# Stick-breaking attention of a hybrid layer: from one query block at a time to steps of two

## The chip, the cores and the metric

The kernel runs on one core of one Trainium2 chip. The metric is the device time of one execution in microseconds (us); lower is better. The core has five engines with an instruction queue each, which meet through semaphores: TensorE (PE in the profile; PEld is its loading of weights), VectorE (DVE), ScalarE (ACT), GpSimd (POOL) and SyncE (SP), which here issues the DMAs. TensorE writes its products to PSUM, and the other engines read them from there.

## What is computed

One layer on 1024 tokens with 16 meta tokens ahead of them, 1024 wide. A normalised input is projected to an SSD mixer and to an attention of 16 heads of 64; both outputs are normalised and go through one W_out of 2048 rows, and a gated feed-forward part follows.

```python
proj = xn @ w_in[l]
...
y_ssd = ssd_mixer(z, xbc, dt_raw, ...)
y_sb = rms_norm(stick_breaking_attention(q, k, v).reshape(Bsz, L, SB_WIDTH), sb_norm_g[l])
mix = jnp.concatenate([y_ssd, y_sb], axis=-1) @ w_out[l]
h = h + rms_norm(mix, mix_post_g[l])
...
f = (jax.nn.gelu(g, approximate=True) * gu[..., D_FF:]) @ w_down[l]
h = h + rms_norm(f, ffn_post_g[l])
```

The attention has no softmax. A key takes the share beta of what the keys after it have left over:

```python
valid = (key_pos[None, :] < q_pos[:, None]) & (key_pos[None, :] >= pad)
zlog = jnp.einsum('bqhd,bkhd->bhqk', qi, kp) * scale
log_beta = jax.nn.log_sigmoid(zlog)
log_keep = jnp.where(valid, log_beta - zlog, 0.0)
after = lax.cumsum(log_keep, axis=3, reverse=True) - log_keep
w = jnp.where(valid, jnp.exp(log_beta + after), 0.0)
return jnp.einsum('bhqk,bkhd->bqhd', w, vp)
```

## The kernel before

The stages follow each other: the input and its projections, the SSD mixer, attention, the output projection, the feed-forward part. The change is in attention and at its seams to the output projection.

Attention runs over eight head pairs `p` (two heads of 64 side by side on TensorE) and, in each, over eight blocks of 128 queries in the order `BLOCKS = (7, 0, 6, 1, 5, 2, 4, 3)`, so that a long block and a short one alternate. Block `i` sees n = 16 + 128(i+1) keys. What is done for one block:

- *Scores*, `block_weights`: q and k are split in a high and a low part, and a score is three products for each head of the pair (z, L1277), in chunks of at most 512 keys (`key_chunks`). ScalarE makes the sigmoid (L1278), and VectorE runs a scan over the keys from the last to the first (L1281), one for each head and chunk, with `hold` as the causal mask. The result is `kp`, what a key leaves over. There are three buffers for long blocks and three for short ones.
- *Corner*, `corner_copy` (L1256): GpSimd puts the first 16 queries' columns of the meta keys' end aside in `cb`.
- *Turns*, `block_turn`, of the block three places earlier (`TURN_LAG`): TensorE transposes `kp` in pieces of 128 keys (tw, L1298); ScalarE copies them as 1-x to `th` (L1303; four buffers).
- *Values*, `block_mix`: products of v and `th` (av, L1316), copied by ScalarE into the head pair's output `ysc` (L1319).
- *Pieces* (`do`): TensorE work from elsewhere, put between the steps above. First come the last pieces of the q and k projections (`plain_steps`, L219; six products of 260 columns each), then the halo rows (`halo_rows`, L1436: two output rows that the convolution further on needs, from the split high and low parts of W_out and in eight rows of four products of 512 columns), then the output projection of the SSD half (`out_steps`, mo, L1471; six products of 512 columns a piece, 64 pieces). `shares`, `FILL_AT` and `OUT_FILL` share a fixed number of pieces out over the 64 blocks; the rest runs after the loop.
- *Edge*, once for each head pair and while the next one is running: the meta keys' part, turned by `edge_turn` (twc L1325, masked by VectorE into thc) at the fourth block, multiplied by `edge_mix` (avc L1336) at the fifth. VectorE adds it to `ysc` (L1339), ScalarE squares the whole head pair for the norm (sqb, L1346), and GpSimd sums the squares.

Scores, turns, avc and other small products share three PSUM buffers of two banks, `psum_zz`; `psum_av` is a buffer of its own. A product into a `psum_zz` buffer must wait until the engine that reads its last content is done.

In the loop each engine's order is the order in which the code is written (`manual_schedule` with all engines), so a wait of one instruction holds up all that stand behind it on that engine. The loop also issues the loads of q (`load_q`, three blocks ahead), of k and v for the next head pair, the stores of finished head pairs (`put_stores`) and the row-wise loads of W_out (`raw_w`), whose rows ACT and POOL split in parts (`wout_steps`). After it the rest of the pieces runs, and with it the second half of W_out is prepared; the second half's halo rows (`halo_raw`, L1649: 32 output columns, from raw rows, four products of 256 columns a row) begin there when the loop counter n is over 11.

Of the kernel before, what the change touches and what calls it, by code (L numbers as in the profile page):

```python
# [9 lines left out]
F32 = mybir.dt.float32  # L10
# [29 lines left out]
OUT_FILL = 14  # L40
FILL_AT = (2, 1)
BLOCKS = (7, 0, 6, 1, 5, 2, 4, 3)
TURN_LAG = 3
# [24 lines left out]
def tile_layer(ctx: ExitStack, tc: tile.TileContext, x, meta, rows, parts,  # L68
# [29 lines left out]
    def psum_av(name):  # L98
        return stage[0][1].tile([P, P], F32, tag="av", name=name, bufs=1)
# [53 lines left out]
    halod = [dr.tile([2, D], F32, name=f"halod{n}", tag=f"halod{n}") for n in range(3)]  # L153
# [1094 lines left out]
    for op_, base, mul, col in ((ALU.is_ge, 0, 1, 0), (ALU.is_ge, NM - 1, -1, 0), (ALU.is_gt, -NM, -1, 1)):  # L1248
        nc.gpsimd.affine_select(out=cmask, in_=cmask, compare_op=op_, fill=0.0, base=base,
                                pattern=[[-NM * mul, NT], [col, 32]], channel_multiplier=mul)  # L1250
    edges, ys_of = {}, {}
# [6 lines left out]
    def block_weights(p, i):  # L1258
        kh, kl = (heads[p][1][:, j] for j in range(2))
        nm = f"{p}_{i}"  # L1260
        q = qs.pop((p, i))
        qh, ql = q[:, 0], q[:, 1]
        if p not in edges:
            edges[p] = ap.tile([P, 2, NT, NM], F32, tag="cb", name=f"cb{p}", bufs=2)
        n = NM + (i + 1) * P
        big = i > 3
        size, tag = (L, "b") if big else (NM + NT * P // 2, "s")
        kpt = ap.tile([P, 2, size], F32, tag="kp" + tag, name=f"kp{nm}", bufs=3)
        kp = kpt[:, :, 0:n]
        m = n - NM  # L1270
        for ci, (a, w) in enumerate(key_chunks(n)[::-1]):
            if ci == 2:
                yield
            z = psum_zz(f"z{nm}_{ci}")
            for s_, (u, r) in enumerate(((qh, kh), (ql, kh), (qh, kl))):
                for h, j in zip(halves, range(2)):
                    mm(z[:, j, :w], u[h, :], r[h, a:a + w], start=s_ == 0, stop=s_ == 2)  # L1277
            nc.scalar.activation(kp[:, :, a:a + w], z[:, :, :w], AF.Sigmoid, scale=-QSCALE)  # L1278
            for j in range(2):
                part = kp[:, j, a:a + w][:, ::-1]  # L1280
                nc.vector.tensor_tensor_scan(part, part, hold[:, L - n + a:L - n + a + w][:, ::-1],  # L1281
                                             1.0 if ci == 0 else kp[:, j, a + w:a + w + 1],
                                             op0=ALU.mult, op1=ALU.max)
            if ci == 0:
                while corner:
                    corner_copy(*corner.pop(0))
        corner.append((p, i, kp, m, n))
        turn.append((p, i, kp))

    def block_turn(p, i, bt, ths):  # L1290
        nm = f"{p}_{i}"
        for u in range(i // 4 + 1):
            nb = min(4, i + 1 - 4 * u)
            tw = psum_zz(f"tw{nm}_{u}").rearrange("p h (b c) -> p h b c", c=P)
            for j in range(2):
                for b in range(nb):
                    c0 = (4 * u + b) * P
                    nc.tensor.transpose(tw[:, j, b, :], bt[:, j, c0:c0 + P], ident)  # L1298
            th = ap.tile([P, 2, 4, P], F32, tag="th", name=f"th{nm}_{u}", bufs=4)
            if u and not left[0]:  # L1300
                nc.vector.tensor_scalar(th[:, :, :nb, :], tw[:, :, :nb, :], -1.0, 1.0, op0=ALU.mult, op1=ALU.add)
            else:
                copied[0] = nc.scalar.activation(th[:, :, :nb, :], tw[:, :, :nb, :], AF.Copy,  # L1303
                                                  scale=-1.0, bias=1.0).ins
            ths.append((nb, th))
        yield

    def block_mix(p, i, ths):
# [1142 lines left out]
```

## Time and profile before

| | |
|---|---|
| runs | 1726.91 us median of 3 (1723.53 to 1729.21) |
| profiled execution | 1729.03 us, its span 1727.2 us |
| granted TensorE clock, mean of the span | 0.989 |
| DMA | 247.40 MB, 143 GB/s over the span |
| scans of kp on DVE (L1281) | 224, 199.7 us |
| sigmoids on ACT (L1278) | 112, 78.5 us |
| copies of turned weights on ACT (L1303) | 96, 74.6 us |
| corner copies on POOL (L1256) | 64, 35.1 us |

The span runs from the first to the last instruction of one execution that a hardware profiler recorded, on the one core. A busy time is the time in which an instruction of that engine is running; TensorE's products overlap each other, so that its busy time is more than what it would need. A group is all instructions of one line and engine, with its count, busy time, mean duration of one, and the idle time of the engine just ahead of them with what ended most of it ("[1.63 <-POOL hold L1243]"). In a window's row a granted clock below 1.00 means that the chip let TensorE run at that share of its full speed.

### The profile page before, as it was taken

What the parts mean: (1) busy time and instruction counts of PE and PEld (TensorE: products, weight loads), DVE (VectorE), ACT (ScalarE), POOL (GpSimd) and SP (SyncE); (2) the same over time, 40 slices, a digit from 0 to 9 for tenths busy, and PEclk for the clock granted to TensorE, in tenths of its full rate; (3) what the DMA queues carried; (4) which work ended last, traced back from release to release, by engine and by line L of the source; (5) the groups of instructions that cost most, each with busy time, mean ns of one, the idle gap of its engine ahead of it and who ended that gap; (6) DMA issues with size and microseconds to landing.
All of it is one profiled execution on the core that took longest, in us unless ns stands there. A gap on an engine that the chain in (4) does not pass through costs nothing.

```text
span 1727.2 us, 29049 instructions
## 1 busy us (share of the span) xinstructions
PE 1673.6 (97%) x11508; PEld 1439.4 (83%) x11508; DVE 1083.7 (63%) x1250; ACT 753.3 (44%) x1146; POOL 770.8 (45%) x580
## 2 busy tenths in 40 slices
PE   5999999999999999999999999999999999999998
PEld 5899999978777787677777788989998888888887
DVE  6776644354366696877750467666566656558777
ACT  6444344232244465766552445423333333344544
POOL 3676856630466462433321222577776777400001
PEclk9999999999999999999999999999999999999999
DMA  5343334334577863543414653222332222396335
GB/s 182 149 145 116 113 123 160 148 128 156 138 225 236 244 214 108 167 132 117 117 49 131 242 174 131 68 105 97 108 106 92 92 92 92 102 329 203 104 104 189
DMA packets 164522, 247.40 MB, mean 143 GB/s; under 512 B 18489, under 2 KB 99489, under 8 KB 162706
## 3 DMA queue, kind: packets, MB, share of 16 engines
q1 hardware_dynamic: 164386, 245.54, 43.8%
q8 instruction: 91, 1.49, 0.4%
q14 instruction: 45, 0.37, 0.1%
HBM read 162.00 MB, written 83.47 MB: 142 GB/s over the span
## 4 chain that ended last, share of the span: by engine, by line
PE 77%; issue 7%; POOL 5%; DMA 4%; DVE 4%; ACT 3%; SPq 1%; POOLq 0%; DVEq 0%; ACTq 0%
PE mo L1471 10%; PE fX L1855 10%; PE dnA L2267 7%; PE fY L1855 6%; PE fA L1855 6%; PE dnB L2267 5%; PE av L1316 3%; PE z L1277 3%; PE tw L1298 3%; PE dXqk L309 2%; PE vB L812 2%; PE pj_k L219 2%; PE dXx L309 2%; PE dYqk L309 1%; PE vA L812 1%
## 5 line engine op out<-in xcount | busy, mean ns | idle before, releaser
L1281 DVE TENSOR_TENSOR_SCAN kp<-kp,hold 128x344 f32<-128x344 f32 (+6 forms) x224 | 199.7, 954 | 76.1 <-ACT kp L1278 73.7
L183 POOL TENSOR_TENSOR wlo<-wr,whi 128x1024 fp32r<-128x1024 f32 x43 | 100.3, 2342 | 40.6 <-ACT whi L182 37.0
L2304 POOL TENSOR_TENSOR fms<-fms 128x1 f32<-128x1 f32 x8 | 2.3, 290 | 222.0 <-ACT dh L2189 195.8
L182 ACT ACTIVATE whi<-wr 128x1024 fp32r<-128x1024 f32 x43 | 45.7, 1063 | 112.7 <-PE fX L1855 73.5
L2189 ACT ACTIVATE dh<-ar 128x512 fp32r<-128x512 f32 x77 | 48.6, 631 | 94.8 <-PE dnB L2267 44.7
L1927 DVE SCALAR_TENSOR_TENSOR ga<-gr,pp,ga 128x1024 f32<-128x1024 f32 x44 | 67.7, 1539 | 33.4 <-ACT ga L1920 32.6
L1303 ACT ACTIVATE th<-tw 128x1024 f32<-128x1024 f32 (+2 forms) x96 | 74.6, 813 | 29.0 <-PE tw L1298 28.5
L1256 POOL TENSOR_SCALAR cb<-kp 128x32 f32<-128x32 f32 x64 | 35.1, 549 | 113.2 <-DVE kp L1281 105.2
L1278 ACT ACTIVATE kp<-z 128x688 f32<-128x688 f32 (+6 forms) x112 | 78.5, 746 | 10.0 <-PE z L1277 9.8
L2190 DVE TENSOR_TENSOR dl<-ar,dh 128x512 fp32r<-128x512 f32 x77 | 53.2, 691 | 47.1 <-ACT dh L2189 47.1
L1316 PEld LDWEIGHTS av<-th,v 128*64 128x64 f32 x1152 | 62.4, 138 | 22.3 <-issue 9.0
L1277 PE MATMUL z<-k,q 64*128 64x348 f32 (+8 forms) x672 | 77.5, 350 | 2.5 <-DVE st L928 1.0
L1298 PE MATMUL tw<-ident,kp 128*128 128x128 f32 x576 | 77.3, 280 | 2.7 <-ACT th L1303 2.7
L1316 PE MATMUL av<-th,v 128*64 128x128 f32 x1152 | 77.8, 280 | 0.5 <-ACT ysc L1319 0.5
L1298 PEld LDWEIGHTS tw<-ident,kp 128*128 128x128 f32 x576 | 62.7, 142 | 12.1 <-issue 7.0
L1277 PEld LDWEIGHTS z<-k,q 64*128 64x128 f32 x672 | 53.0, 189 | 20.9 <-issue 9.5
L2267 PE MATMUL dnA<-dl,dh 128*128 128x512 f32 x176 | 68.5, 389 | 0.0
L2267 PE MATMUL dnA<-dh 128*128 128x512 f32 x176 | 68.5, 389 | 0.0
L2267 PE MATMUL dnA<-dh,dl 128*128 128x512 f32 x176 | 68.5, 389 | 0.0
L1988 POOL TENSOR_TENSOR al<-wr,ah 128x512 fp32r<-128x512 f32 x20 | 28.6, 1432 | 81.6 <-ACT ah L1987 81.5
L498 DVE SCALAR_TENSOR_TENSOR cdX<-craw_x,pp,cdX 128x1040 f32<-128x1040 f32 x24 | 51.6, 2149 | 0.6
L2267 PE MATMUL dnB<-dh 128*128 128x512 f32 x132 | 51.3, 389 | 0.0
(998 smaller groups left out, 6058.9 us busy)
## 6 DMA issues: line engine op xcount, KB each, us to landing
wr<-in_w_up SPq DMA_DIRECT2D x44, 512.0 KB
fds<-ga SPq DMA_DIRECT2D x44, 256.0 KB
b<-in_w_down SPq DMA_DIRECT2D x44, 256.0 KB
ar<-fds SPq DMA_DIRECT2D x44, 256.0 KB
fda<-ga SPq DMA_DIRECT2D x33, 256.0 KB
ar<-fda SPq DMA_DIRECT2D x33, 256.0 KB
k<-qkd SPq DMA_DIRECT2D x8, 1040.0 KB
q<-qkd SPq DMA_DIRECT2D x64, 128.0 KB
```

What stands on the lines that cost most here:

```text
L183: nc.gpsimd.tensor_tensor(l, raw, h.bitcast(F32), op=ALU.subtract)
L309: mm(acc[:, c, :CQ], u[:, k, :], v[:, k, c * CQ:(c + 1) * CQ], start=first and k == 0 and j == 0, stop=k == 3 and j == 2, skip_group_check ...
L1277: mm(z[:, j, :w], u[h, :], r[h, a:a + w], start=s_ == 0, stop=s_ == 2)
L1278: nc.scalar.activation(kp[:, :, a:a + w], z[:, :, :w], AF.Sigmoid, scale=-QSCALE)
L1281: nc.vector.tensor_tensor_scan(part, part, hold[:, L - n + a:L - n + a + w][:, ::-1], 1.0 if ci == 0 else kp[:, j, a + w:a + w + 1], op0=A ...
L1298: nc.tensor.transpose(tw[:, j, b, :], bt[:, j, c0:c0 + P], ident)
L1303: copied[0] = nc.scalar.activation(th[:, :, :nb, :], tw[:, :, :nb, :], AF.Copy, scale=-1.0, bias=1.0).ins
L1316: mm(av[halves[j], :], v[:, kb, halves[j]], th[:, j, b, :], start=kb == 0, stop=kb == i)
L1471: recent[0] = mm(acc, u[:, k, :], v[:, cs], start=(k == 0 and j == 0), stop=(k == 7 and j == 2))
L1855: mm(acc[:, c, :nn], u[:, k, :], v[:, k, c0:c0 + nn], start=first and k == 0 and j == 0, stop=k == 3 and j == 2, skip_group_check=not first)
L1927: nc.vector.scalar_tensor_tensor(v, self.g[jj][:, :, i:i + 256], fconv_w[:, j, i:i + 1], v, op0=ALU.mult, op1=ALU.add)
L2267: mm(banks[BANK[n], t], u[:, 0, c], v[:, 1, :], start=(n in (1, 2, 5) and p == 0 and i == 0), stop=(p == NPR - 1 and i == 2), skip_group_c ...
```

## The change

Two blocks that follow each other in `BLOCKS` make one step: 32 steps, `p` = step // 4, `m` = step % 4. Both blocks' keys lie one behind the other in one `kp` (two buffers), and `CUTS` cuts them into three chunks, so that a sigmoid may cover the end of one block and the beginning of the other. A step is now written as: scores of both (`pair_weights`), values of the pair turned a step earlier (`pair_mix`; both blocks in one bank, one copy), turns of the pair before (`pair_turn`), a fixed number of pieces (`FILLS`). The edge's product shares the bank of the values: at m = 2 it stands behind them (`edge_sum`), and its add and square follow the copy (`edge_mix`); `edge_turn` is at m = 1. The table `extras` places what else is to be done. The first half's halo rows are made as the second half's were: raw rows of W_out (four buffers) times `y0w`, which is y with the gain and 32 columns (30 of them zero), two rows in a group, 256 columns a product, the four groups summed by VectorE in `mh0`; one intermediate in DRAM (`halod`) is gone, and one step of `halo_sum` with it. q is loaded for the next pair only. The load of the meta values goes later, `pick` is made earlier, and the second half's halo rows may begin at n > 5.

```diff
-OUT_FILL = 14
-FILL_AT = (2, 1)
+FILLS = (4,) + 8 * (2,) + 23 * (1,)
 BLOCKS = (7, 0, 6, 1, 5, 2, 4, 3)
-TURN_LAG = 3
+CUTS = ((788, 394), (728, 272), (792, 400), (788, 394))
...
-        return stage[0][1].tile([P, P], F32, tag="av", name=name, bufs=1)
+        return stage[0][1].tile([P, 4, P], F32, tag="av", name=name, bufs=1)
...
+    def pair_weights(p, m):
         kh, kl = (heads[p][1][:, j] for j in range(2))
+        nm = f"{p}_{m}"
         if p not in edges:
             edges[p] = ap.tile([P, 2, NT, NM], F32, tag="cb", name=f"cb{p}", bufs=2)
+        blocks = BLOCKS[2 * m:2 * m + 2]
+        sizes = [NM + (i + 1) * P for i in blocks]
+        bases = [sizes[1], 0]
+        total = sum(sizes)
+        kp = ap.tile([P, 2, total], F32, tag="kp", name=f"kp{nm}", bufs=2)
+        q = [qs.pop((p, i)) for i in blocks]
+        top = total
+        for ci, lo in enumerate(CUTS[m] + (0,)):
             z = psum_zz(f"z{nm}_{ci}")
+            parts = [(x, max(lo, b), min(top, b + n)) for x, (b, n) in enumerate(zip(bases, sizes))
+                     if max(lo, b) < min(top, b + n)]
+            for x, a, e in parts:
+                qh, ql = q[x][:, 0], q[x][:, 1]
+                for s_, (u, r) in enumerate(((qh, kh), (ql, kh), (qh, kl))):
+                    for h, j in zip(halves, range(2)):
+                        mm(z[:, j, a - lo:e - lo], u[h, :], r[h, a - bases[x]:e - bases[x]], start=s_ == 0, stop=s_ == 2)
+            nc.scalar.activation(kp[:, :, lo:top], z[:, :, :top - lo], AF.Sigmoid, scale=-QSCALE)
+            for x, a, e in parts:
+                last = bases[x] + sizes[x]
+                for j in range(2):
+                    part = kp[:, j, a:e][:, ::-1]
+                    nc.vector.tensor_tensor_scan(part, part, hold[:, L - last + a:L - last + e][:, ::-1],
+                                                 1.0 if e == last else kp[:, j, e:e + 1],
+                                                 op0=ALU.mult, op1=ALU.max)
+            top = lo
+        for i, b, n in zip(blocks, bases, sizes):
+            corner.append((p, i, kp, b + n - NM, b + n))
+        turn.append((p, blocks, bases, kp))
...
+    def pair_turn(p, blocks, bases, kp):
+        ths = []
+        for i, base in zip(blocks, bases):
+            mine = []
+            for u in range(i // 4 + 1):
+                nb = min(4, i + 1 - 4 * u)
+                tw = psum_zz(f"tw{p}_{i}_{u}").rearrange("p h (b c) -> p h b c", c=P)
+                for j in range(2):
+                    for b in range(nb):
+                        c0 = base + (4 * u + b) * P
+                        nc.tensor.transpose(tw[:, j, b, :], kp[:, j, c0:c0 + P], ident)
+                th = ap.tile([P, 2, 4, P], F32, tag="th", name=f"th{p}_{i}_{u}", bufs=4)
+                if u and not left[0]:
+                    nc.vector.tensor_scalar(th[:, :, :nb, :], tw[:, :, :nb, :], -1.0, 1.0, op0=ALU.mult, op1=ALU.add)
+                else:
+                    copied[0] = nc.scalar.activation(th[:, :, :nb, :], tw[:, :, :nb, :], AF.Copy,
+                                                      scale=-1.0, bias=1.0).ins
+                mine.append((nb, th))
+            ths.append((i, mine))
+        mix.append((p, ths))
...
+    def pair_mix(p, both, av, last=None):
         v = heads[p][2]
         if p not in ys_of:
             ys_of[p] = ap.tile([P, NT, P], F32, tag="ysc", name=f"ysc{p}", bufs=2)
+        for x, (i, ths) in enumerate(both):
+            for u, (nb, th) in enumerate(ths):
+                for b in range(nb):
+                    kb = 4 * u + b
+                    for j in range(2):
+                        mm(av[halves[j], 1 - x, :], v[:, kb, halves[j]], th[:, j, b, :], start=kb == 0, stop=kb == i)
+        hi, lo = both[0][0], both[1][0]
+        if last:
+            edge_sum(*last, av)
+        nc.scalar.activation(ys_of[p][:, lo:hi + 1:hi - lo, :], av[:, 0:2, :], AF.Copy)
+        if last:
+            edge_mix(last[0], av)
...
+    y0w = ap.tile([P, 8, 32], F32, tag="y0w", name="y0w")
+    nc.gpsimd.memset(y0w, 0.0)
+    nc.gpsimd.tensor_tensor(y0w[:, :, 0:2], y0a, ssd_g.unsqueeze(2).to_broadcast([P, 8, 2]), op=ALU.mult)
+    mh0 = ap.tile([P, 256], F32, tag="mh0", name="mh0")
...
-    shares = [FILL_AT[i % 2] * (4 if i < 2 else 1) for i in range(8 * NT)]
-    total = 2 * (64 - 11 - SCAN_FILL) + 9 + 2 * OUT_FILL
-
-    def share(n):
-        return round(total * sum(shares[:n]) / sum(shares))
...
+    rawt = []
+
+    def load_rows(n):
+        for k in range(len(rawt), len(rawt) + n):
+            rawt.append(raw_w(0, k, ap.tile([P, D], F32, tag="wor", name=f"wora{k}", bufs=4)))
+            raws0.append(rawt[-1])
+
+    def halo_go(r):
+        acc = psum_zz(f"halo{r}")[:, 0, 0:256]
+        for k in (2 * r, 2 * r + 1):
+            for c in range(4):
+                mm(acc[32 * c:32 * c + 32, :], y0w[:, k, :], rawt[k][:, 256 * c:256 * c + 256],
+                   start=k == 2 * r, stop=k == 2 * r + 1)
+        if r == 0:
+            nc.vector.tensor_copy(mh0, acc)
+        else:
+            nc.vector.tensor_tensor(mh0, acc, mh0, op=ALU.add)
+        if r == 3:
+            for c in range(4):
+                nc.sync.dma_start(out=halod[0][:, 256 * c:256 * c + 256], in_=mh0[32 * c:32 * c + 2])
+
+    def load_y0():
+        taken[0] += 1
+        raws0y.append(load_y(0, taken[0], yraw[0](f"yk0_{taken[0]}")))
+
+    def split_y0():
+        ys1.append(split_y(wp, 0, len(ys1) + 1, ("whi", "wlo", WB), raws0y.pop(0), nc.vector))
+
+    def row():
+        run(wsteps, 1)
+
+    extras = {(1, 0): lambda: do(4), (1, 2): lambda: load_rows(2), (2, 0): lambda: load_rows(2), (3, 2): lambda: (halo_go(0), row()),
+              (4, 0): row, (4, 2): lambda: (halo_go(1), row(), load_rows(2)),
+              (5, 0): lambda: (row(), load_rows(2)), (5, 2): load_y0, (6, 0): load_y0, (6, 2): lambda: halo_go(2),
+              (7, 0): split_y0, (7, 2): lambda: (halo_go(3), split_y0()), (8, 2): row, (9, 2): row, (10, 2): row,
+              (11, 2): row}
...
+    for step in range(4 * 8):
+        p, m = step // 4, step % 4
+        if step:
+            load_q(2 * step + 2)
+        load_q(2 * step + 3)
+        if m == 3:
             put_stores()
+        while corner:
+            corner_copy(*corner.pop(0))
+        pair_weights(p, m)
+        if p == 0 and m < 2:
+            run(vsteps, 2 - m)
+        if len(mix):
+            av = psum_av(f"av{step}")
+            pair_mix(*mix.pop(0), av, p > 0 and m == 2 and (p - 1, edge))
+        if m == 0:
             load_k(p + 1)
+            if p:
+                next(vsteps, None)
+        elif p < 7:
+            if m == 2:
+                vsteps = load_v(p + 1)
+            else:
+                meta_of(p + 1 if m == 3 else 0) if m == 3 or p == 0 else None
+            if m > 1:
+                next(vsteps, None)
+        extra(step, 0)
+        if len(turn) > 1:
+            pair_turn(*turn.pop(0))
+        do(FILLS[step])
+        if p > 0 and m == 1:
             edge = edge_turn(p - 1)
...
+    pair_mix(*mix.pop(0), psum_av("av32"))
+    do(1)
+    pair_turn(*turn.pop(0))
+    do(4)
     edge = edge_turn(7)
+    av = psum_av("av33")
+    pair_mix(*mix.pop(0), av, (7, edge))
...
-            while n > 11 and len(summed) < rows_in:
+            while n > 5 and len(summed) < rows_in:
```

What this makes of the order on TensorE, at the output projection's first row block: the rows of before, head pair 5, from a piece of mo0_2_0 to the next one. A row is line, operation, output and inputs (av values, tw turns, z scores, mo a piece; the number behind av, tw and z is the head pair, the next the block), size of the output and how often it stands in a row.

```order
L1471 MATMUL mo0_2_0_8647<-woabxl_7645,yh0_2_7762 128x512
L1316 MATMUL av5_7_8824<-th5_7_0_8732,v5_8387 64x128 x8
L1316 MATMUL av5_7_8824<-th5_7_1_8743,v5_8387 64x128 x8
L1298 MATMUL tw5_6_0_8850<-ident_69,kp5_6_8681 128x128 x8
L1298 MATMUL tw5_6_1_8861<-ident_69,kp5_6_8681 128x128 x6
L1277 MATMUL z5_2_0_8871<-k5_8207,q5_2_8668 128x400 x6
L1316 MATMUL av5_0_8882<-th5_0_0_8784,v5_8387 64x128 x2
L1298 MATMUL tw5_1_0_8893<-ident_69,kp5_1_8745 128x128 x4
L1277 MATMUL z5_4_0_8901<-k5_8207,q5_4_8721 128x328 x6
L1277 MATMUL z5_4_1_8912<-k5_8207,q5_4_8721 128x328 x6
L1471 MATMUL mo0_2_1_8922<-woab11h_6552,yh0_2_7762 128x512
```

The rows after, head pair 4, its last step, from a piece to the next one (z4_3_1 is the step's second chunk, which the two blocks share).

```order
L1471 MATMUL mo0_2_0_8289<-woab21l_6932,yh0_2_7243 128x512
L1279 MATMUL z4_3_0_8414<-k4_7748,q4_4_8304 128x396 x6
L1279 MATMUL z4_3_1_8424<-k4_7748,q4_4_8304 128x260 x6
L1279 MATMUL z4_3_1_8424<-k4_7748,q4_3_8306 128x134 x6
L1279 MATMUL z4_3_2_8442<-k4_7748,q4_3_8306 128x394 x6
L1323 MATMUL av19_8452<-th4_6_0_8382,v4_7950 64x128 x8
L1323 MATMUL av19_8452<-th4_6_1_8391,v4_7950 64x128 x6
L1323 MATMUL av19_8452<-th4_1_0_8398,v4_7950 64x128 x4
L1303 MATMUL tw4_5_0_8479<-ident_69,kp4_2_8310 128x128 x8
L1303 MATMUL tw4_5_1_8490<-ident_69,kp4_2_8310 128x128 x4
L1303 MATMUL tw4_2_0_8497<-ident_69,kp4_2_8310 128x128 x6
L1471 MATMUL mo0_2_0_8289<-woab22h_7362,yh0_2_7243 128x512
```

Values, turns and scores of single blocks came in turn between two pieces; now each kind stands together once in a step.

The order on VectorE around the edge. Before, in head pair 5 (thc and the add of ysc are the edge of head pair 4; the scans L1281 and after the change L1285 have this name in the order of the program):

```order
L1281 SCALAR_TENSOR_TENSOR kp5_1_8745<-kp5_1_8745,hold_6267 128x272 x2
L1328 TENSOR_TENSOR thc4_8776<-twc4_8773,cmask_6271 128x256 x2
L1281 SCALAR_TENSOR_TENSOR kp5_5_8786<-kp5_5_8786,hold_6267 128x392 x4
L1339 TENSOR_TENSOR ysc4_8385<-avc4_8808,ysc4_8385 128x8x32
L1281 SCALAR_TENSOR_TENSOR kp5_2_8870<-kp5_2_8870,hold_6267 128x400 x2
```

After, in head pair 4 with the edge of head pair 3 (kp4_2 is the step of the edge, with three chunks):

```order
L1285 SCALAR_TENSOR_TENSOR kp4_1_8211<-kp4_1_8211,hold_6266 128x272 x2
L1338 TENSOR_TENSOR thc3_8301<-twc3_8298,cmask_6270 128x256 x2
L1285 SCALAR_TENSOR_TENSOR kp4_2_8310<-kp4_2_8310,hold_6266 128x392 x4
L1285 SCALAR_TENSOR_TENSOR kp4_2_8310<-kp4_2_8310,hold_6266 128x400 x2
L1352 TENSOR_TENSOR ysc3_7924<-av18_8341,ysc3_7924 128x8x32
```

Ahead of the add in its step stood the four scans of one block; now it is all six of the pair.

The order on ScalarE at the same two places, before and after (sqb is the square of the head pair, ma a copy of a piece, ysc that of the values, th those of the turned weights, kp the sigmoids):

```order
L1278 ACTIVATE kp5_5_8786<-z5_5_0_8787 128x2x392
L1278 ACTIVATE kp5_5_8786<-z5_5_1_8798 128x2x392
L1346 ACTIVATE sqb4_8812<-ysc4_8385 128x1024
L1484 ACTIVATE ma2_0_8821<-mo0_2_0_8647,r_ssd_88 128x512
L1319 ACTIVATE ysc5_8841<-av5_7_8824 128x128
L1303 ACTIVATE th5_6_0_8859<-tw5_6_0_8850 128x1024
L1303 ACTIVATE th5_6_1_8868<-tw5_6_1_8861 128x2x384
```

```order
L1280 ACTIVATE kp4_2_8310<-z4_2_0_8311 128x2x392
L1280 ACTIVATE kp4_2_8310<-z4_2_1_8321 128x2x392
L1280 ACTIVATE kp4_2_8310<-z4_2_2_8331 128x2x400
L1327 ACTIVATE ysc4_8342<-av18_8341 128x2x128
L1359 ACTIVATE sqb3_8365<-ysc3_7924 128x1024
L1308 ACTIVATE th4_6_0_8382<-tw4_6_0_8373 128x1024
L1308 ACTIVATE th4_6_1_8391<-tw4_6_1_8384 128x2x384
L1308 ACTIVATE th4_1_0_8398<-tw4_1_0_8393 128x2x256
L1280 ACTIVATE kp4_3_8413<-z4_3_0_8414 128x2x396
```

The square stood ahead of two copies of th, those of one block; it now stands behind all of the step's sigmoids and the copy of the values, and ahead of three copies of th.

More of the change, by code (lines that the diff above doesn't have):

```diff
@@ L1290, in block_turn @@
[L1290 to L1306, printed above, removed]
@@ L1496, in tile_layer @@
     taken = [0]
-    def begin_turn():
-        tp_, ti, bt = turn.pop(0)
-        ths = []
-        mix.append((tp_, ti, ths))
-        steps = block_turn(tp_, ti, bt, ths)
-        next(steps, None)
-        return steps
     meta_steps = attend_meta()
@@ L1592, in tile_layer @@
             run(meta_steps, 1)
-        if p == 0 and n == 3:
+        if p == 0 and m == 1:
             run(token_rstd(r_ssd, ap, "a", psum_zz("pta")[:, 0, :]))
-    while turn or mix:
-        due = mix[:1]
-        if turn:
-            run(begin_turn())
-        do(4)
-        for d in due:
-            mix.remove(d)
-            block_mix(*d)
+    while corner:
+        corner_copy(*corner.pop(0))
+    pair_mix(*mix.pop(0), psum_av("av32"))
+    do(1)
+    pair_turn(*turn.pop(0))
+    do(4)
```

136 lines of the change are left out of this document (21 added, 115 removed).

## The prediction

> **What bounds the kernel now.** I read the page first, then the table by windows for the stretch in which the edited loop stands, then TensorE's own timeline in that stretch, and last what the other engines do around one wait.
>
> ```profile
> span 1727.2 us, 29049 instructions
> PE 1673.6 (97%) x11508; PEld 1439.4 (83%) x11508; DVE 1083.7 (63%) x1250; ACT 753.3 (44%) x1146; POOL 770.8 (45%) x580
> ...
> 598.42:996.48 398.06, 389.49 (x3295) 300.03 (x3295) 248.24 (x295) 219.99 (x354) 135.86 (x146) 0.99 0.46 143
> ```
>
> The last row is the stretch from the first score product of attention to the first turn of the next stage (window, its length, then busy time of PE, PEld, DVE, ACT, POOL). PE is busy in 389.5 of 398.1 us, and has the same work before and after except eight halo rows. So an idle gap cannot be where much is won. But busy time hides what a change of the array's shape costs, and that shows in the starts:
>
> ```profile
> 790.75 0.50 PE L1471 MATMUL mo<-woab21h,yh 128*128 128x512 f32 x1
> ...
> 791.80 0.39 PE L1471 MATMUL mo<-woab21l,yl 128*128 128x512 f32 x1
> 792.03 0.40 PE L1471 MATMUL mo<-woab21l,yh 128*128 128x512 f32 x1
> 792.36 1.31 PE L1316 MATMUL av<-th,v 128*64 128x128 f32 x20
> 793.60 1.97 PE L1298 MATMUL tw<-ident,kp 128*128 128x128 f32 x16
> 795.50 0.64 PE L1277 MATMUL z<-k,q 64*128 64x272 f32 x6
> ...
> 802.78 1.97 PE L1316 MATMUL av<-th,v 128*64 128x128 f32 x32
> 804.68 1.75 PE L1298 MATMUL tw<-ident,kp 128*128 128x128 f32 x14
> ...
> 813.24 1.53 PE L1298 MATMUL tw<-ident,kp 128*128 128x128 f32 x12
> 814.70 0.51 PE L1277 MATMUL z<-k,q 64*128 64x264 f32 x4
> ...
> 902.19 0.87 PE L1298 MATMUL tw<-ident,kp 128*128 128x128 f32 x6
> 902.82 0.47 PE L1471 MATMUL mo<-woab11h,yh 128*128 128x512 f32 x1
> ```
>
> Columns are start, busy time, engine, line, operation, operands, array rows*columns, count. Two mo start 0.23 apart; from the first of six to the next run are 1.61, that is 0.22 more than 6 x 0.232. Twenty av records take 1.24 and thirty-two take 1.90, so 0.055 each and 0.14 over. Sixteen tw take 1.90, twelve 1.46: 0.11 each and 0.14 over. Each run of another shape thus costs 0.14 to 0.22, mean 0.17. Where the shape stays 128*128, from tw to mo at 902, six tw take 0.63: nothing over.
>
> **The change part by part.** *Pairing.* In PE's row order from the first score to the end of that stretch I count 275 changes of shape before and 116 after: a step of two blocks now goes scores, values, turns, piece, with three changes (turn to piece is free), where each single block had three or four. 159 x 0.17 = **-27.0 us**. As a check of the method: pricing every record of before at its pitch and every change at its 0.14 to 0.22 gives 382.7 of the measured 398.1, so **15.4 us** are true waits and half-rate clock, which the new order replaces with its own (below).
>
> *Scores in chunks cut over the pair.* Still fourteen pieces a head, but one has 134 columns where the six products cannot run below about 0.11 a pair: +0.13 x 8 = **+1.0**. Fewer, longer sigmoids (96 for 112) and copies of values (32 for 64) lie on ACT, beside PE's work, and are costed at nothing as ACT is busy 220 of 398; uncovered they would be a gain, not a cost.
>
> *Halo rows.* These move from split rows to raw ones, with 256 columns for 512.
>
> ```profile
> 719.96 1.04 PE L1436 MATMUL halo<-woab22h,y 128*2 128x512 f32 x8
> 720.93 1.09 PE L1316 MATMUL av<-th,v 128*64 128x128 f32 x16
> ```
>
> A row takes 0.97 to the next run's start, 0.80 without its change of shape (those are counted above); half the columns make 0.40: 8 x 0.40 = **-3.2**. That 32 output columns instead of 2 cost the same is not shown; between 0 and +3.2, I take 0, since the full 128 columns of the mo and tw rows above show no load of weights between products.
>
> *The pieces.* 24 pieces of q/k projection are still done in the loop; of the output projection 28 pieces stand inside attention and its end, for 48 before. The rest runs on at the same 0.23 pitch: nothing. Raw rows, two loads of y and q now wait in SP's queue behind row copies and stores; q is issued one pair ahead (about 7.7 us) instead of three blocks. No row shows PE waiting for q, so 0, at worst 1 us on a few steps. The second half's halo rows start earlier and may meet their loads: 0 to 1, I take 0.5.
>
> *The start.* The new first turn comes after the second pair's scores and four pieces, PE reaching it at about 598.4 + 1.8 + 3.1 + 1.9 + 3.0 = 608.2.
>
> ```profile
> 602.86 9.37 DVE L1281 TENSOR_TENSOR_SCAN kp<-kp,hold 128x344 f32<-128x344 f32 x10 [1.63 <-POOL hold L1243]
> ```
>
> Six scans of the first block, of ten in 9.37, are done near 609.7: **+1.7** (0 to 3).
>
> *The edge step.* Once a head (seven times in the loop, at its third pair) the meta edge is added. Before, this is the order of one such place:
>
> ```profile
> 799.28 1.41 PE L1277 MATMUL z<-k,q 64*128 64x392 f32 x12
> ...
> 800.17 1.54 ACT L1278 ACTIVATE kp<-z 128x784 f32<-128x784 f32 x2 [0.34 <-PE z L1277]
> ...
> 801.03 3.69 DVE L1281 TENSOR_TENSOR_SCAN kp<-kp,hold 128x392 f32<-128x392 f32 x4 [1.11 <-ACT kp L1278]
> ...
> 804.63 0.40 DVE L1339 TENSOR_TENSOR ysc<-avc,ysc 128x256 f32<-128x256 f32 x1
> ...
> 805.13 1.06 ACT L1346 ACTIVATE sqb<-ysc 128x1024 f32<-128x1024 f32 x1 [3.42 <-DVE ysc L1339]
> ...
> 806.82 1.72 ACT L1303 ACTIVATE th<-tw 128x1024 f32<-128x1024 f32 x2
> ...
> 807.90 0.66 PE L1298 MATMUL tw<-ident,kp 128*128 128x128 f32 x4 [0.35 <-ACT th L1303]
> ```
>
> The square (L1346) waits on ACT for DVE's add, which stands behind the scans; the copies of turned weights (L1303) wait behind the square, and PE for them. After the change six scans stand ahead of the add, not four, and all three copies of the pair behind the square. From the step's first score, T: first sigmoid T+0.9, scans from T+1.75, six at 0.92 to 0.95, add at T+7.25 to 7.65, square T+7.75 to 8.8, copies done T+9.74, 10.5 and 11.0 (1.02 for four blocks of keys by its group, and by that for three and two about 0.8 and 0.6):
>
> ```profile
> L1303 ACT ACTIVATE th<-tw 128x1024 f32<-128x1024 f32 x48 | 48.3, 1023 | 20.8 <-PE tw L1298 20.7
> ```
>
> PE in that step: scores 1.8, values 2.1 with the edge's 0.5, turns 2.1, piece 1.4, so it wants the next scores at T+7.96; their three banks come free only with those copies. It then starts its values at T+11.75 instead of 9.76: 2.0 lost. Five times 2.0, 1.5 for the first head (its step also has a halo group), 2.9 for the second (a row copy adds to both engines): **+14.4**, bounds 0 (the add overtaken by nothing I see) and 20.
>
> *The clock.* One wait of before was followed by half rate (window, length, busy PE, PEld, DVE, ACT, POOL, then granted clock):
>
> ```profile
> 689.60:693.03 3.43, 1.83 (x16) 1.10 (x14) 0.56 (x1) 3.41 (x6) 2.27 (x1) 1.00 0.69 182
> 693.04:699.86 6.82, 6.46 (x40) 4.08 (x42) 6.15 (x5) 4.64 (x8) 4.88 (x5) 0.50 0.73 216
> ```
>
> A window of 3.4 us with 1.6 us without PE work was followed by 6.8 us at 0.50, which lose half, 3.4; one window alone would lose 1.7. A wait of 1.9 lies with 1.6 of it in one such window if it starts in 2.1 of each 3.4 us, so four or five of the seven: about 4.5 x 1.8 = **+8**, bounds 0 and 17 (five of 3.4). The Trainium skill ("TensorE: Matmul & The Clock Gate", Part 1) has the clock fall after a whole window of about 3.4 us idle; by it these waits would cost no clock and the sum would be 8 less. The rows above disagree: PE was busy 1.83 of 3.43 in the window ahead.
>
> *Sum* against the profiled execution, 1729.0 us (span 1727.2 and 1.8 around it): -27.0 - 15.4 - 3.2 + 1.0 + 0.5 + 1.7 + 14.4 + 8 + 0.5 for the loop's end = -19.5, so 1709.5. The median of the runs is 2.1 lower; from it 1707.4. I take **1708**.
>
> **The rivals.** *The edge wait does not bite* (the add gets through earlier, or PE has other work left): then 14.4 and most of 8 go, 1727 - 40 = 1687 to 1700. For it: no view shows the new order. Against it: the same chain cost PE in before. *More waits than I see*, in SP's queue or in GpSimd's corner copies, which now hold one of two kp buffers: 8 to 14 more, 1716 to 1722. *The cover was worth as much as the changes* (the change does not do what it says): single blocks let the piece hide each latency; if each pair lost 1 us, 31 us, the gain would be gone: 1722 to 1732. *Slower: ScalarE becomes the bound.* It alone empties every bank of scores and turns; if its last copy came late in every step as in the edge step, 31 x 2.0 and the clock, 1727 - 41 + 62 = 1748. It decides where PE waits over 1.4 us in each step. Against it: by the groups a pair asks ACT for 2.5 + 2.4 + 0.4 and some 0.6 of other work, 6 of 7.7 us, and in an ordinary step the first copy is out near T+5.9, two us ahead. The Trainium skill ("TensorEngine Tiling (Array Packing)", PSUM Bottleneck) warns that emptying PSUM may become the bottleneck of packed products and asks for ScalarE and VectorE both; this rival is that rule taken whole.
>
> **How the numbers follow.** My forecast, 1700 to 1716, has 0.50. The edge wait missing has 0.17, more waits 0.15, no gain 0.10, ScalarE's bound 0.08. Range 1686 to 1722, which leaves out the slower cases and a little of each end. A measurement of this kernel tells about 0.3%, 5 us, from no change: faster 0.82, same 0.10, slower 0.08.
>
> **What would show it.** In the new profile a turn run should go into mo with no gap over pitch, and an ordinary pair step take some 7.7 us. Each third pair of a head should show the square idle for 3 us or more behind DVE's add and PE waiting about 1.9 for a copy, often with a 0.50 window behind it. I am wrong if PE waits in ordinary steps too, if DVE's scans of a pair pass 7.7 us, or if the three changes of shape in a step cost more than 0.5 together.

## The result and the profile after

The changed kernel takes 1699.03 us, the median of 4 runs (1695.74 to 1701.05), against 1728.06 us before (4 runs, 1723.53 to 1729.92). The ratio is 0.983, with an interval of 0.981 to 0.986. The forecast was 1708 with a range of 1686 to 1722. So the number lies 9 us below the forecast, a touch under the 1700 to 1716 that had half of the chance, and inside the 1687 to 1700 of the first rival, whose mechanism the trace refutes.

The line of engines on the page of the changed kernel (span 1697.4 us), and its row for the same stretch as before (window, length, busy time of PE, PEld, DVE, ACT, POOL, granted clock):

```profile
PE 1641.2 (97%) x11508; PEld 1442.9 (85%) x11508; DVE 1084.5 (64%) x1253; ACT 746.4 (44%) x1094; POOL 765.9 (45%) x582
...
595.76:971.19 375.43, 359.13 (x3295) 304.72 (x3296) 249.12 (x298) 213.42 (x302) 131.14 (x148) 0.98 0.49 151
```

TensorE is still busy 97% of the span, with as many records (11508). The stretch went from 398.06 to 375.43, 22.6 us less, and TensorE's busy time in it from 389.49 to 359.13: 30.4 us of "work" went away although no product did except through the halo rows. What went is time between the starts of products, which a busy time holds too, since the profile models the ends of products. TensorE now is idle for 16.3 us of the stretch, twice the 8.6 of before: the change pays with new waits. (Below, a "wait" of TensorE is an idle time of more than 0.15 us, as the profile lists them; they sum to 17.2 and 8.8 us.)

TensorE's timeline of two ordinary steps shows what a step is now.

```profile
768.35 1.98 PE L1279 MATMUL z<-k,q 64*128 64x396 f32 x24
770.25 2.19 PE L1323 MATMUL av<-th,v 128*64 128x128 f32 x36
772.37 2.18 PE L1303 MATMUL tw<-ident,kp 128*128 128x128 f32 x18
774.31 0.48 PE L1471 MATMUL mo<-woabxh,yh 128*128 128x512 f32 x1
...
775.88 1.89 PE L1279 MATMUL z<-k,q 64*128 64x456 f32 x18
777.71 2.19 PE L1323 MATMUL av<-th,v 128*64 128x128 f32 x36
779.82 2.19 PE L1303 MATMUL tw<-ident,kp 128*128 128x128 f32 x18
781.76 0.48 PE L1471 MATMUL mo<-woab11h,yh 128*128 128x512 f32 x1
```

A step takes 7.53 us (768.35 to 775.88), where 7.7 was expected; 18 turns run into the piece in 1.94, 0.108 each, so that this boundary costs nothing. No wait stands in these rows.

The third step of a head pair is another matter. Here are TensorE, then VectorE, then ScalarE around the edge of one head pair:

```profile
783.56 1.87 PE L1279 MATMUL z<-k,q 64*128 64x392 f32 x18
785.36 2.19 PE L1323 MATMUL av<-th,v 128*64 128x128 f32 x36
...
793.14 3.15 PE L1279 MATMUL z<-k,q 64*128 64x396 f32 x24 [1.66 <-ACT th L1308]
...
785.32 5.46 DVE L1285 TENSOR_TENSOR_SCAN kp<-kp,hold 128x392 f32<-128x392 f32 x6 [0.90 <-ACT kp L1280]
790.69 0.40 DVE L1352 TENSOR_TENSOR ysc<-av,ysc 128x256 f32<-128x256 f32 x1
...
791.12 1.06 ACT L1359 ACTIVATE sqb<-ysc 128x1024 f32<-128x1024 f32 x1 [2.71 <-DVE ysc L1352]
792.09 2.19 ACT L1308 ACTIVATE th<-tw 128x1024 f32<-128x1024 f32 x3
```

From the step's first score, 783.56, the add comes 7.13 us later, behind six scans; the square waits 2.71 for it, three copies stand behind the square, and TensorE waits 1.66 for the first of them. The view of waits over the stretch adds them up (engine and line, what it waited for, us, times, longest):

```profile
ACT sqb L1359 <- DVE ysc L1352: 16.5, 7, 3.0
...
PE z L1279 <- ACT th L1308: 9.7, 6, 2.0
PE z L1279 <- DMA q<-qkd: 3.0, 1, 3.0
```

The windows around three waits, one near the start and two at edges, and the windows behind two of them:

```profile
609.80:613.21 3.41, 2.05 (x19) 1.93 (x18) 3.41 (x4) 0.00 (x0) 3.26 (x4) 1.00 0.95 302
613.22:620.03 6.81, 5.18 (x36) 4.74 (x38) 4.01 (x9) 2.48 (x3) 3.60 (x5) 0.50 1.08 345
691.70:695.10 3.40, 1.77 (x10) 1.16 (x8) 1.68 (x3) 1.69 (x2) 0.55 (x1) 1.00 1.10 301
790.65:794.06 3.41, 1.75 (x12) 1.05 (x12) 0.44 (x2) 2.94 (x4) 1.80 (x1) 1.00 1.03 288
794.07:797.47 3.40, 3.40 (x30) 2.94 (x30) 1.49 (x1) 3.31 (x5) 2.74 (x2) 0.51 0.37 110
```

The edge at 791 was followed by a window at half rate, and the one at 825 by another; the window at 691.70, with as little work of TensorE, was not. Near the start the half rate set in while TensorE waited for q, and lasted two windows; TensorE was busy in 5.18 of their 6.81 us, so it lost half of that, 2.6.

### The profile page after: what moved, and what is told of

It reads as the page before. It is cut to its first block, busy times and chain, and to the rows that moved or that the text cites. A ratio compares the mean times of both kernels' runs of the same rounds, so it can differ in the third digit from the quotient of the medians.

```text
span 1697.4 us, 28962 instructions
## 1 busy us (share of the span) xinstructions
PE 1641.2 (97%) x11508; PEld 1442.9 (85%) x11508; DVE 1084.5 (64%) x1253; ACT 746.4 (44%) x1094; POOL 765.9 (45%) x582
## 4 chain that ended last, share of the span: by engine, by line
PE 81%; issue 6%; DVE 5%; POOL 3%; DMA 2%; ACT 2%; SPq 1%; POOLq 0%; DVEq 0%; ACTq 0%
PE fX L1861 10%; PE mo L1471 10%; PE dnA L2273 7%; PE fY L1861 7%; PE fA L1861 7%; PE dnB L2273 5%; DVE kp L1285 3%; PE av L1323 3%; PE z L1279 3%; PE tw L1303 2%; PE pj_k L218 2%; PE dXqk L308 2%; PE pj_q L218 2%; PE vB L811 2%; PE vA L811 2%
## 5 line engine op out<-in xcount | busy, mean ns | idle before, releaser
L1285 DVE TENSOR_TENSOR_SCAN kp<-kp,hold 128x396 f32<-128x396 f32 (+5 forms) x224 | 197.1, 949 | 43.5 <-ACT kp L1280 41.7
L1280 ACT ACTIVATE kp<-z 128x788 f32<-128x788 f32 (+4 forms) x96 | 73.6, 835 | 23.6 <-PE z L1279 19.7
L1279 PE MATMUL z<-k,q 64*128 64x396 f32 (+9 forms) x672 | 68.1, 345 | 15.1 <-ACT th L1308 9.7
L1308 ACT ACTIVATE th<-tw 128x1024 f32<-128x1024 f32 (+2 forms) x96 | 70.7, 811 | 14.0 <-PE tw L1303 12.6
L1323 PE MATMUL av<-th,v 128*64 128x128 f32 x1152 | 72.1, 281 | 0.0
L1303 PE MATMUL tw<-ident,kp 128*128 128x128 f32 x576 | 70.0, 276 | 0.5 <-DVE kp L1285 0.5
L2273 PE MATMUL dnB<-dl,dh 128*128 128x512 f32 x132 | 51.4, 390 | 0.0
```

Of the source, the lines that this page charges most:

```text
L1279: mm(z[:, j, a - lo:e - lo], u[h, :], r[h, a - bases[x]:e - bases[x]], start=s_ == 0, stop=s_ == 2)
L1280: nc.scalar.activation(kp[:, :, lo:top], z[:, :, :top - lo], AF.Sigmoid, scale=-QSCALE)
L1285: nc.vector.tensor_tensor_scan(part, part, hold[:, L - last + a:L - last + e][:, ::-1], 1.0 if e == last else kp[:, j, e:e + 1], op0=ALU.m ...
L1303: nc.tensor.transpose(tw[:, j, b, :], kp[:, j, c0:c0 + P], ident)
L1323: mm(av[halves[j], 1 - x, :], v[:, kb, halves[j]], th[:, j, b, :], start=kb == 0, stop=kb == i)
L2273: mm(banks[BANK[n], t], u[:, 0, c], v[:, 1, :], start=(n in (1, 2, 5) and p == 0 and i == 0), stop=(p == NPR - 1 and i == 2), skip_group_c ...
```

## The experiments

**A change of shape, measured by itself.** Eight small products are added between turns and piece in 18 steps, once with the two shapes in turn, once in two groups. The edit, of which the other kernel has `[0] * 4 + [1] * 4`:

```diff
             pair_turn(*turn.pop(0))
+        if step > 7 and m != 2:
+            kd = heads[p][1][:, 0]
+            for full in [0, 1] * 4:
+                rows_ = slice(0, P) if full else halves[0]
+                mm(av[:, 3, 0:64], kd[rows_, 0:P], kd[rows_, 0:64], start=True, stop=True)
         do(FILLS[step])
```

> The changed kernel with eight small products of 64 columns added between turns and piece in 18 of its steps, none of them read by anything: four on 64 rows of the array and four on 128, in turn, so that each step has eight changes of shape there. Theory (a change of shape costs 0.14 to 0.22 whatever work is around it): 18 x 6 x 0.17 = 18 us more than the same eight products in two groups, in which a step has two changes. Rival (the gaps before were waits of engines, which pairing hid; a change of shape itself costs nothing): both kernels agree within 3 us.

> The same eight products in the same 18 steps, four on 64 rows first and then four on 128. Theory: 18 us less than the kernel that mixes them, and over the changed kernel 18 x (2 x 0.17 + 8 x 0.05) = 13 us, which is an estimate from the values' 0.055 a product. Rival: the same time as the mixed one.

Measured: 1736.60 mixed (1734.18 to 1738.72) and 1723.53 grouped (1720.65 to 1727.88), 13.1 us apart. The first two rows are TensorE's timeline of the mixed kernel, the last two that of the grouped one.

```profile
799.94 1.88 PE L1600 MATMUL av<-k 64*128 64x64 f32 x8
801.65 0.47 PE L1471 MATMUL mo<-woab11h,yh 128*128 128x512 f32 x1
```

```profile
792.85 1.19 PE L1600 MATMUL av<-k 64*128 64x64 f32 x8
793.88 0.47 PE L1471 MATMUL mo<-woab11h,yh 128*128 128x512 f32 x1
```

The same eight products take 1.71 us to the piece in one order and 1.03 in the other. Six changes more cost 0.68, so **0.114 us each** between products this small; all 18 steps show the same two times, and 18 x 0.68 = 12.3 us. That the medians come so near to it is in part chance: of the 13.5 us between the two traces 8.8 lie in the stretch, where the grouped kernel has five windows at half rate and the mixed one three, and 4.7 outside it. The two times in place carry the result: a change costs time with nothing else changed, and the rival falls; but it costs less here than the 0.14 to 0.22 of the prediction. The grouped kernel was also dearer than expected, 24.5 us over the changed kernel for 13. From its last turn to the piece it takes 1.23 us where the changed kernel takes 0.11, because products of 64 columns followed each other after some 0.11 us, not 0.05; 18 x 1.12 is 20.2 of the 24.5. Its five windows at half rate explain little, since the changed kernel's trace has four.

**The pairs taken apart.** In the kernel with the late square (below), each step is taken apart on TensorE; products and buffers stay. The three functions hand back between their parts (`yield`, not shown), and the loop calls the parts in turn.

```diff
-        pair_weights(p, m)
...
+        before = turn.pop(0) if turn else None
+        weights = pair_weights(p, m)
+        next(weights)
...
+            mixing = pair_mix(*mix.pop(0), av, p > 0 and m == 2 and (p - 1, edge))
+            next(mixing)
+        if before:
+            turning = pair_turn(*before)
+            next(turning)
+        run(weights)
...
+            run(mixing)
...
+        if turning:
+            run(turning)
```

> The kernel with the late square, but each step of two blocks taken apart again on TensorE: two chunks of scores, values of the long block, its turns, the third chunk, values of the short block, its turns, the piece. The same products, six changes of shape in a step for three, so about 29 x 3 = 87 more. Theory: 87 x 0.14 to 0.22 = 12 to 19 us over the late square's 1689, that is 1701 to 1708, by the changes alone, with no more waits in the trace. Rival (pairing gained by hiding waits, and changes cost little): 0 to 6 us, 1689 to 1695. By the 0.114 that the small products gave it would be 10 us, 1699.

Measured: 1699.39 (1698.97 to 1700.25), 10.3 over the late square's 1689.05: less than the theory's 12 to 19, more than the rival's 0 to 6. One step of each, taken apart first, then in pairs:

```profile
746.25 1.51 PE L1281 MATMUL z<-k,q 64*128 64x456 f32 x12
747.69 1.31 PE L1326 MATMUL av<-th,v 128*64 128x128 f32 x20
748.94 1.96 PE L1305 MATMUL tw<-ident,kp 128*128 128x128 f32 x16
750.83 0.64 PE L1281 MATMUL z<-k,q 64*128 64x272 f32 x6
751.40 1.09 PE L1326 MATMUL av<-th,v 128*64 128x128 f32 x16
752.42 0.44 PE L1305 MATMUL tw<-ident,kp 128*128 128x128 f32 x2
752.62 0.48 PE L1483 MATMUL mo<-woab11h,yh 128*128 128x512 f32 x1
```

```profile
741.33 1.88 PE L1279 MATMUL z<-k,q 64*128 64x456 f32 x18
743.14 2.19 PE L1323 MATMUL av<-th,v 128*64 128x128 f32 x36
745.25 2.19 PE L1303 MATMUL tw<-ident,kp 128*128 128x128 f32 x18
747.19 0.48 PE L1478 MATMUL mo<-woab11h,yh 128*128 128x512 f32 x1
```

The same 72 records take 6.37 us apart and 5.86 in pairs: 0.51 for three changes, **0.17 each**. In most ordinary steps the difference is 0.44 to 0.51, 0.15 to 0.17 a change. The records of the two stretches change shape 209 and 117 times; 92 x 0.16 = 14.7, of which 10.2 arrived (374.2 for 364.1 us). Most of the rest came back in two ways. TensorE's waits sum to 7.2 us for 9.0: the late square still has 0.81, 0.25, 1.31 and 0.62 in its steps with an edge, which the taken-apart order does not have, so that one of these steps is 1.1 us shorter apart, while near the start apart waits longer. And it has one window at half rate for two, 1.4 us. Without waits and half rate the stretches differ by 13.4 us, 0.15 a change. So both readings hold: the changes make the sum, and single blocks did hide some latency, 2 to 3 us.

**The square behind the copies.** The add and the square of the edge come apart, and ScalarE's square goes behind the pair's copies of turned weights.

```diff
         stores.append((yd1[:, :, p, :].rearrange("t d c -> d t c"), ysc))
+        whole[0] = p, ysc
...
+    def edge_square():
+        p, ysc = whole[0]
+        whole[0] = None
         flat = ysc.rearrange("p t c -> p (t c)")
...
             pair_turn(*turn.pop(0))
+        if whole[0]:
+            edge_square()
         do(FILLS[step])
...
     pair_mix(*mix.pop(0), av, (7, edge))
+    edge_square()
```

> The changed kernel, with the head pair's square on ScalarE issued behind the copies of the pair's turned weights and no longer ahead of them. Theory: TensorE's wait once a head (the trace gives 9.7 us in 6 waits for the copies of th) is the square's wait for VectorE's add, so it goes, and so does the half clock that followed two of the waits (3.4 us at 0.50 each, 1.7 lost each): 10 to 15 us, 1684 to 1689 for 1699, and no 0.50 window in the loop except near its start. Rival: ScalarE as a whole is the bound at that place, and the wait moves to the next sigmoids or to the next step: 0 to 4 us, 1695 to 1699.

Measured: 1689.05 (1688.25 to 1689.33), 10.0 less, the edge of what the theory gives; 8.7 less if each is set against the kernel before as it ran beside it (1726.74 here, 1728.06 above). ScalarE and TensorE behind the same edge:

```profile
786.09 2.22 ACT L1308 ACTIVATE th<-tw 128x1024 f32<-128x1024 f32 x3 [0.69 <-PE tw L1303]
788.17 1.07 ACT L1366 ACTIVATE sqb<-ysc 128x1024 f32<-128x1024 f32 x1
...
788.41 2.03 PE L1279 MATMUL z<-k,q 64*128 64x396 f32 x24
```

The copies wait for the turns alone, the square has its sum when it comes, and the next scores start with no wait. Not every edge gains so much: at this one (head pair 5) the step goes from 9.59 to 7.86 us, in head pair 3 only from 9.59 to 9.45, with another wait of 1.31 in it. The stretch takes 364.07 for 375.43, 11.3 less, of which the two windows at half rate at edges were 3.4; behind 622 us it has none. So moving the square, clock included, was worth 9 to 11 us, and ScalarE as a whole was not the bound there.

**q earlier.** The third pair's q is loaded in the first step.

```diff
-        if step:
+        if step > 1:
             load_q(2 * step + 2)
-        load_q(2 * step + 3)
+        if step != 1:
+            load_q(2 * step + 3)
...
         pair_weights(p, m)
+        if step == 0:
+            load_q(4)
+            load_q(5)
```

> The changed kernel, with the third pair's two loads of q issued in the first step ahead of the loads of v, not at the head of the second step behind them. Theory: the 3.0 us that TensorE waits for q in the third step and the half clock behind it (6.8 us at 0.50, 3.4 lost) both go: 1692 to 1693. Rival: another wait takes its place (the scans of the first pairs on VectorE are late anyway): the half clock stays, 0 to 3 us, 1696 to 1699.

Measured: 1696.45 (1692.36 to 1701.43), which the runs alone don't tell from 1699.03. The trace shows the third pair's wait gone and others in its place (0.24 ahead of its last chunk; 1.7 for the split of a projection piece), and the waits at the edges as before:

```profile
PE z L1279 <- ACT th L1308: 9.6, 6, 2.0
PE pj_q L218 <- ACT sw L924: 1.7, 1, 1.7
...
615.52 1.37 PE L1279 MATMUL z<-k,q 64*128 64x400 f32 x6 [0.24 <-PE z L1279]
...
614.90:618.30 3.40, 3.16 (x24) 2.34 (x22) 3.10 (x7) 2.22 (x3) 3.32 (x4) 0.50 1.02 388
```

One window at half rate is left of two near the start, and the stretch is 5.5 us shorter in the one trace, 369.9. But 3.4 of that is not the work of q: the edges wait as long as in the changed kernel, and in this trace none of them is followed by half rate. Up to the fourth step's first score the trace gains 2.3 us (26.6 for 28.9). So the rival, 0 to 3 us, is the nearer one.

**Both together.** 

> Late square and early q together. If they are independent: 10.0 and 2.6 us off 1699, so 1686; if the half clock near the start stays whatever is done to q, 1689 as with the late square alone.

Measured: 1685.53 (1684.74 to 1687.87), the lowest median here, 0.977 of before (0.975 to 0.979). Every run lies under every run of the late square alone, by a small margin: the kernel before took 1725.66 beside this one and 1726.74 beside that one. The median fits the first expectation; the trace does not show why. Its half rate near the start is still there, two windows from 614.71 us, and its stretch is 363.0 for the late square's 364.1.

**The rest of the start and the edge.** Two more edits on top: the sums of the SSD half's norm two steps later (`m == 3` for `m == 1`), and with it the edge's turns into the free half of the bank of the values (`tw = av[:, 2:4]`).

> Late square, early q, and the sums for the norm of the SSD half (18 small products into pta, read by VectorE) two steps later, in the fourth step. Theory: with q early, what still holds TensorE near the start is the third chunk of scores, 1.3 us in the trace: its PSUM buffer is that of pta, which VectorE reads only behind 14 scans. In the fourth step VectorE has no such queue: the 1.3 us go, and with them perhaps the 6.8 us at 0.50 behind (3.4 lost): 1681 to 1684 for 1685.5. Rival: the half clock there comes from TensorE's small products and earlier waits together, and stays: 1684 to 1686.

> As before, and the turns of the edge go to the free half of the bank of the values, no longer to a buffer of the scores. Theory: the third chunk of scores in each head's third step waited for VectorE to read that buffer behind its scans (0.6 to 0.8 us in 3 or 4 heads, 1.8 us in all): 1 to 2 us less than the kernel with late sums. Rival: the values then wait for the same reading at the next step: no difference.

Measured: 1689.07 (1684.74 to 1694.46) and 1685.68 (1683.22 to 1689.05), against 1685.53. Neither is a gain over the two fixes. With late sums a load of q held TensorE again, a step later:

```profile
620.42 3.22 PE L1279 MATMUL z<-k,q 64*128 64x396 f32 x24 [1.92 <-DMA q<-qkd]
```

Against late sums alone the last edit has a median 3.4 us lower where 1 to 2 were expected, but the runs with late sums spread over 10 us. The trace with all edits has a stretch of 358.4 us without a window at half rate, but it is of the fastest of four runs, which spread over 6 us: near the start one wait takes the place of another.

**The kernel before, traced again.** 

> The kernel before, unchanged, for a second trace. In the first pair of traces 7.3 of the 29.8 us of difference lie outside the stretch of attention and its output projection: 2.7 ahead of it, 4.6 behind it (a wait of 2.8 us for VectorE where the feed-forward part begins, with half clock behind it). Theory: that is the chance of single runs, so that this trace shows other numbers there (131 to 134 us from the first turn of the next stage to that place) and the stretch itself within 1 to 2 us of 398.1. Rival: the edit shifted the feed-forward part's transfers, and the wait stands here as in the first trace, 133.6.

Measured: 1725.07, with a stretch of

```profile
596.60:996.27 399.67, 390.89 (x3295) 301.40 (x3296) 248.71 (x295) 219.99 (x354) 133.91 (x146) 0.98 0.46 142
```

From the first turn of the next stage to the first product of the feed-forward part that waited for VectorE (2.78 us in the first trace, 0.48 in this one) it has 131.3 us, for 133.6 in the first trace; the changed kernel has 130.6. Outside the stretch its span has 1723.1 - 399.7 = 1323.4 us, the first trace 1329.1, the changed kernel 1322.0. So 5.7 of the 7.1 us outside were the chance of that one execution, and what the edit does in its stretch is 22.6 and 24.2 by the two traces of before. The 29.0 between the medians is likely some us too large: beside the later kernels the kernel before took 1726.74, 1725.66 and 1725.13 (medians of 13, 7 and 9 runs) for 1728.06.

## Why the prediction was right, and where not

- **Changes of shape, -27.0: right.** TensorE's records change shape 275 and 117 times, and in place a change cost 0.15 to 0.17: 158 x 0.16 = -25.3. That a price read from starts is a price of its own, not a hidden wait, is what the small products show for changes between 64 and 128 rows, and the taken-apart steps for all kinds together. The Trainium skill ("TensorEngine Tiling (Array Packing)", Key Properties) says that a change of tiling mode drains TensorE, without a price; the runs agree that a change costs time, 0.114 us between small products and 0.16 between these, and don't show what the time goes into. From turns to piece, at one shape, it is nothing.
- **The old waits go, -15.4: nearly right.** In the first trace of before TensorE's waits sum to 8.8 us, and it lost 4.9 at half rate (half of the 9.87 in which it was busy then), 13.7 together. No run takes them away one by one. The second trace of before has the half rate at both places again (from 692.7 and 890.7), so it went with the old order; the changed kernel has none there. Two of the waits did not go: 0.99 ahead of the first scores, and that for VectorE's add behind the last edge, 0.70 before and 0.97 after.
- **The halo rows, -3.2: right.** A group of two rows in the changed kernel's timeline:

```profile
659.59 1.07 PE L1537 MATMUL halo<-wora,y0w 128*32 128x256 f32 x16 [0.71 <-ACT th L1308]
660.59 2.03 PE L1279 MATMUL z<-k,q 64*128 64x396 f32 x24
```

  It takes 1.00 us from start to start, so 4.0 for eight rows, where one row took 0.97. That 32 output columns cost nothing holds.
- **The edge step, +14.4 and the clock, +8: the mechanism right, the size too large.** The add at T+7.13 (7.25 to 7.65 expected), the wait of the square of 2.71 (3 or more expected) and TensorE's 1.66 (2.0) are the chain as drawn. But TensorE's waits for the copies are 9.7 us, with the 0.7 ahead of a halo group at the first of the seven edges 10.4, for 14.4; and only two of seven edges fell to half rate, one window each, 3.4 us for 8. In the trace with q early the same waits brought no half rate at all, so the 3.4 is itself the chance of an execution. This is the term that was mis-sized most, by some 9 us.
- **The start, +1.7: too small.** The wait for the first pair's scans was 0.53. Beside it q came late, 3.0 us, which the prediction set at 0 because no row of before showed TensorE waiting for q, though it had named the shorter lead and the queue. The two windows at half rate cost 2.6. About +6 in all.
- **The sum: partly luck.** The traces can be split without any price. Waits and the loss at half rate are 8.8 + 4.9 us of the stretch before and 17.2 + 6.0 after; what is left is 384.3 and 352.2. So waits with clock rose by 9.5, and the prediction's terms for them (-15.4 + 1.7 + 14.4 + 8) give +8.7. That this fits is luck: the edge and its clock were taken some 9 us too large, the start some 4 too small, and waits that the sum does not have (0.99 at the first scores, 0.81 in a third step, 0.97 at the end and two smaller ones) make up most of the rest. What is left fell by 32.1, where the prediction's other terms give 28.2. Of these 32.1 the prices measured here explain about 27 (25.3 for the changes and 3.2 for the halo rows, less the 1.5 that the prediction puts on the scores and the second half's halo rows, which no run measured); the other 5 was not taken apart.
- The rivals: *the edge wait does not bite* is refuted by the trace, *ScalarE becomes the bound* by the late square. *More waits than I see* came in part, with the load of q, without reaching its 1716 to 1722. *The cover was worth as much as the changes* is refuted in size, but the taken-apart steps show that it exists.

## What to carry to other kernels

A tensor engine that is 97% busy may still lose time between products (here 275 x 0.16 = 44 us of a stretch of 398): count the changes of array shape in its order, and price one by the starts of a run and of the next. Grouping work by shape saves them, and it moves buffers and other engines' queues; look there for the one step in each round in which an instruction off the bound engine stands ahead of those that it waits for. Here a square one place too early on ScalarE cost about 10 us where the grouping had brought 25 or more, and moving it was a few lines.

## What was not expected of the hardware

- The half rate does not follow from TensorE's busy share of one window alone: 1.83 of 3.43 us (before, at 689.60) and 1.75 of 3.41 were followed by it, 1.77 of 3.40 was not. With q early an edge with 1.75 of 3.41 (789.00 to 792.41) was not followed by it either, behind the same products and the same wait of 1.66. The windows lie on a grid: in the changed kernel's trace the half rate begins at 613.22, 794.12 and 828.26 us, 53.0 and 10.0 times 3.413 us apart. What else counts stays open. The Trainium skill ("TensorE: Matmul & The Clock Gate", Part 1) asks for a whole idle window, which none of them was. One such window is in the taken-apart kernel's trace (604.72 to 608.13, no product), and half rate followed it too.
- Half the columns did not make a product cheaper here: 64 columns on 64 or on 128 rows followed each other after 0.11 us, as the turns of 128 columns do, while the values, 128 columns on half of the array's columns, follow after 0.055. What sets the 0.11 was not tested.
- Runs of the changed kernel go with the clock: the run of 1695.74 has a mean granted clock of 0.993, that of 1701.05 one of 0.988. 0.005 of 1697 us is 8.5 us of clock for 5.3 us of time. It does not hold for each pair of runs: of the kernel before one run of 0.993 took 1725.12 and one of 0.989 took 1725.13.
